# First feed-forward product of quarters 2 to 4 by Strassen's algorithm, with weight sums made in DRAM

## Chip, cores and metric

The kernel runs on one core of a Trainium2 chip (trn2). The metric is the device time of one execution in microseconds (us), median of three runs; TensorE is called PE, VectorE DVE, ScalarE ACT, GpSimd POOL and SyncE SP, as in the profile.

## What is computed

One layer of a streaming encoder on a residual stream x of 512 frames by 1024 channels: a root-mean-square norm, one wide projection, three gated branches (gated linear attention, forgetting attention, attention into 256 memory tokens), a merge with an output projection, and then the feed-forward part, which the change rewrites:

```python
u2 = rmsnorm(h, g_ffn[l])
h = h + jnp.square(jax.nn.relu(u2 @ w_ff1[l])) @ w_ff2[l]
...
return rmsnorm(h, g_final)
```

Here `u2` is 512 x 1024, `w_ff1` 1024 x 4096 and `w_ff2` 4096 x 1024, all float32.

## The kernel before

**Numbers in two halves.** Every large float32 product is made of three PE passes. An operand is split into a rounded half `hi` and a rest `lo`: `split` (L174 to L176) and `split_w` (L112 to L117) make `hi` by a cast on ACT and `lo` by a subtraction on DVE. `mm3` (L122 to L125) then issues hi times hi, hi times lo and lo times hi into one PSUM bank. In the profile these are the lines L123, L124 and L125.

**Weights.** The host lays all weights out as chunks of 128 x 1024 float32 (512 KB), in the order of `chunk_list` (L33). `load_w` (L106) fetches a chunk on SP's queue into one of three `raw` buffers; the halves go into three `hi` and three `lo` buffers of the pool `weights`. A cast therefore waits until PE has finished with the chunk three places back. The matmuls are in the order of the program text; the order on the other engines, their DMA issues included, is set by the framework's planner, and each engine works through its own list strictly in that order.

**Stages.** Memory projection, forgetting attention (`fox_*`, with its projections woven in by `weave`), memory attention woven with the first gated branch, linear attention (`pool("gla")`, L641) woven with the second, then the third branch and the output projection `w_out` (L790 to L851), and then the feed-forward part (from L861). POOL has little to do: in the linear attention it takes the powers in `rsqrt` (L203), clears score tiles (L716) and adds up branches (L571); later it takes the powers of `rms_tile` (L785) and issues accumulating DMAs (L931, L960).

**Into the feed-forward part.** `u2_turn(t)` (L825) transposes the normed rows of one 128-frame tile on PE in two groups and splits each group into `u2h` and `u2l` straight from PSUM. `half` (L836) makes the first two 128-channel tiles of the first product in two halves of 256 frames, so that PE has work while the last frames are normed.

**The feed-forward part** is cut into four quarters of 1024 hidden channels (L983). In each quarter the first product is eight channel tiles, each one weight chunk and 24 matmuls with the weights standing in the array and 512 frames moving (`gT`, L127). `act_evac` (L880) applies relu and square on ACT, forms the seven left factors that the second product needs (L895) and splits them into `ch` and `cl`. Then `second(q)` (L949) makes the second product by Strassen's algorithm: seven products in the order 1, 2, 5, 6, 7, 4, 3, each made of two chunks (called i = 0 and 1) and two row tiles (t), that is 24 matmuls with 512 moving columns; products 1 and 5 stay in PSUM over the quarters. The right factors are sums of blocks of `w_ff2`, and `factor` (L955) forms them in place: POOL issues a DMA that adds a second block from DRAM onto the raw block (L960), and `split_b` (L870) splits the result. Product 6 uses the same raw block as product 5, so its DMA can be issued only when product 5's split has read it. `split_b` puts every fourth chunk into a pair of its own (`bhi`, `blo`), so that a chunk's halves are free again after four chunks.

**The end.** `evac` (L914) adds the products onto the residual rows `hN`; in the last quarter some of these additions are accumulating DMAs (L931). `finish` (L899) makes the sum of squares on ACT, the power on POOL and the scaled output on DVE (L905), and sends two halves out on two queues. Product 3 is last, so the rows t = 0 and 1 are the last to be finished.

Of the kernel before, what the change touches and what calls it, by code (L numbers as in the profile page):

```python
# [32 lines left out]
def chunk_list():  # L33
# [28 lines left out]
def hybrid_block(ctx, tc, chunks, wst, xT, memT, xN, cols, gffn, gfin, wup, cst, out):  # L62
# [42 lines left out]

    def load_w(key, eng=None):  # L106
        i = index[key]
        raw = wp.tile([P, 1024], F32, tag="raw", name=nm("raw"))
        (eng or nc.sync).dma_start(raw, wst[i])
        return raw  # L110

    def split_w(raw):  # L112
        hi = wp.tile([P, 1024], F32R, tag="hi", name=nm("whi"))
        lo = wp.tile([P, 1024], F32R, tag="lo", name=nm("wlo"))
        nc.scalar.copy(hi, raw)  # L115
        nc.vector.tensor_tensor(lo, raw, f(hi), op=ALU.subtract)  # L116
        return hi, lo  # L117
# [670 lines left out]
    u2h = up.tile([P, KT, S], F32R, tag="uhi", name="u2h")  # L788
    u2l = up.tile([P, KT, S], F32R, tag="ulo", name="u2l")
    with pool("outp") as op_:  # L790
# [4 lines left out]
        run(branch("gate_gla", "w_gla_o", ogh, ogl, 2, last=(mh, ml)))  # L795

# [28 lines left out]
        def u2_turn(t):  # L825
            for g in range(2):
# [3 lines left out]
                sl = slice(t * P, (t + 1) * P)  # L830
                last = split(u2h[:, 4 * g:4 * g + 4, sl], u2l[:, 4 * g:4 * g + 4, sl], pt)
# [4 lines left out]
        def half(j, i, ks=range(KT)):  # L836
            sl = slice(256 * i, 256 * i + 256)
            for k in ks:
                mm3(first[j][:, sl], ws[j][0][:, k, :], ws[j][1][:, k, :], u2h[:, k, sl], u2l[:, k, sl], k == 0, k == KT - 1)
# [12 lines left out]
    mst.close()  # L852
# [7 lines left out]

    with pool("ff") as yp:  # L861
        R6, R7 = ([yp.tile([P, 512], F32, name=f"R{n}{t}") for t in range(2)] for n in (6, 7))
        NQ = 4
        held = {}
        split_n = [0]

        def scratch():
            return yp.tile([P, S], F32, tag="sq", name=nm("sq"), bufs=3)

        def split_b(raw):  # L870
            split_n[0] += 1
            own = split_n[0] % 4 == 0
# [3 lines left out]
            return [t.rearrange("p (k c) -> p k c", k=2) for t in (hi, lo)]  # L876

        A = []

        def act_evac(ps):  # L880

            sq = scratch()
            nc.scalar.activation(sq, ps, AF.Relu)
            nc.scalar.activation(sq, sq, AF.Square)
            if not A or A[-1][2] is not None:
                h, l = (yp.tile([P, 7, 256], F32R, tag=g, name=nm(g), bufs=4) for g in ("ch", "cl"))
                split(h[:, 0, :], l[:, 0, :], sq[:, :256])
                A.append([h, l, None, sq])
                return
            h, l, _, sa = A[-1]  # L890
            A[-1][2] = sq
            split(h[:, 1:3, :], l[:, 1:3, :], sq.rearrange("p (a t) -> p a t", a=2))
            ss = yp.tile([P, 4, 256], F32, tag="ss", name=nm("ss"))
            a11, a21, a12, a22 = sa[:, :256], sa[:, 256:], sq[:, :256], sq[:, 256:]
            for o, x, y in ((0, a21, a22), (2, a11, a21), (1, a11, ss[:, 0, :]), (3, a12, ss[:, 1, :])):  # L895
                nc.vector.tensor_tensor(ss[:, o, :], x, y, op=ALU.subtract)
            split(h[:, 3:7, :], l[:, 3:7, :], ss)

        def finish(t, c, n):  # L899
            sumsq(scratch(), hN[t], t, c, n)  # L900
            if n == 1:
                r = rms_tile(yp, t)
                for g, eng in ((0, nc.scalar), (1, nc.sync)):
                    gs_ = slice(512 * g, 512 * g + 512)
                    nc.vector.scalar_tensor_tensor(hN[t][:, gs_], hN[t][:, gs_], r, gl[:, gs_], op0=ALU.mult, op1=ALU.mult)  # L905
                    eng.dma_start(out[t * P:(t + 1) * P, gs_], hN[t][:, gs_])
# [4 lines left out]
        def add(to, x, op=ALU.add):  # L911
            nc.vector.tensor_tensor(to, to, x, op=op)

        def evac(q, n, t, ps):  # L914
            last = q == NQ - 1
            if n == 1 and last:
                add(C(0, 0, t), ps)
            if n in (6, 7):
# [5 lines left out]
            if n == 6 and last:  # L924
                if t == 0:
                    held["G"] = yp.tile([P, 2, 512], F32, tag="ss", name=nm("G"))
                E, G = R6[t], held["G"][:, t, :]
                nc.vector.tensor_tensor(E, held[1][t], R6[t], op=ALU.subtract)
                nc.vector.tensor_tensor(G, held[5][t], E, op=ALU.subtract)
                for to, x in ((C(1, 0, t), E), (C(1, 1, t), G), (C(0, 1, t), G)):  # L930
                    nc.gpsimd.dma_start(to, x, accum_op=ALU.add)  # L931
            if n == 7 and last:
                add(C(1, 1, t), R7[t], ALU.subtract)
                finish(2 + t, 1, 0)
                add(C(1, 0, t), R7[t])
# [4 lines left out]
            if n == 3:  # L940
                add(C(0, 1, t), ps)
                if last:
                    finish(t, 1, 1)
            if n == 2:
                add(C(0, 0, t), ps)
                if last:
# [133 lines left out]
```

## Time and profile before

| what | value |
|---|---|
| median of 3 runs | 864.08 us (863.69 to 866.55) |
| time of the profiled execution | 865.53 us |
| its span, first to last instruction | 863.7 us |
| PE busy | 847.6 us (98%) |
| DVE, ACT, POOL busy | 493.8 (57%), 403.4 (47%), 88.3 us (10%) |
| granted PE clock, mean | 0.992 |
| first product of the third quarter (from 691.23 us of the span on) | 43.52 us |
| second product of the second quarter (from 653.15 us on) | 38.08 us |

The profiled execution lies 1.8 us above its own span and 1.4 us above the median. A matmul row shows a duration that overlaps with its neighbours, since matmuls are pipelined; what counts is the distance from one start to the next. "Busy" of PE in a window is the covered time, not the work done. A bracket at the end of a row of the time line gives the engine's idle time before that instruction and what ended it.

### The profile page before, as it was taken

The page shows a single profiled execution, that of the slowest core. Times are in us where ns is not written, and L with a number is a line of the kernel's source. Part 1 is how long each engine was busy: PE and PEld are TensorE (multiplying, and loading weights), DVE is VectorE, ACT ScalarE, POOL GpSimd, SP SyncE. Part 2 cuts the span into 40 slices and gives each one's busy share as a digit, 9 for nine tenths or more (in the row PEclk, how much of TensorE's full clock was granted, in tenths as well). Part 3 has the DMA queues.
Part 4 walks back from the last instruction along what each step waited for, and adds up shares of the span by engine and source line. Part 5 has one row for each costly group of instructions (what it writes and reads, how often), then busy time and mean ns, then how long its engine had stood idle before and what let it go on. Part 6 is the DMA issues. An engine that isn't in the chain of part 4 may idle for free.

```text
span 863.7 us, 10684 instructions
## 1 busy us (share of the span) xinstructions
PE 847.6 (98%) x4081; PEld 700.0 (81%) x4081; DVE 493.8 (57%) x812; ACT 403.4 (47%) x640; POOL 88.3 (10%) x96
## 2 busy tenths in 40 slices
PE   8999999999999999999999999999999999999995
PEld 5878788888888888787888889888888888888884
DVE  5684556746444546475443446665556645665577
ACT  7665746745243332232333334655455345535642
POOL 5100000000000011212122100011001100110022
PEclk8999999999999999999999999999999999999999
DMA  8333222221221222124332422958625933791156
GB/s 327 123 112 118 91 98 86 90 76 62 92 92 62 90 74 82 41 74 160 109 122 97 146 74 83 352 113 199 204 83 123 278 126 79 145 276 62 25 104 164
DMA packets 31938, 106.10 MB, mean 123 GB/s; under 512 B 3824, under 2 KB 4624, under 8 KB 31888
## 3 DMA queue, kind: packets, MB, share of 16 engines
q1 hardware_dynamic: 24624, 83.92, 27.2%
q0 software_dynamic: 5472, 18.35, 12.0%
q10 hardware_dynamic: 1792, 3.16, 1.0%
q8 instruction: 32, 0.52, 0.3%
q14 instruction: 18, 0.15, 0.1%
HBM read 101.73 MB, written 2.11 MB: 120 GB/s over the span
## 4 chain that ended last, share of the span: by engine, by line
PE 92%; DVE 3%; ACT 1%; DMA 1%; issue 1%; SPq 0%; POOL 0%; DVEq 0%; POOLq 0%; ACTq 0%
PE mm L123 25%; PE mm L124 25%; PE mm L125 25%; PE a L124 3%; PE a L125 3%; PE a L123 3%; PE a L720 1%; PE a L449 1%; DMA h<-G 1%; DMA cst_s<-in_cst_dram 1%; PE a L737 1%; PE a L480 1%; PE a L479 1%; PE a L731 1%; PE a L447 1%
## 5 line engine op out<-in xcount | busy, mean ns | idle before, releaser
L116 DVE TENSOR_TENSOR wlo<-raw,whi 128x1024 fp32r<-128x1024 f32 x104 | 131.1, 1263 | 141.4 <-ACT whi L115 138.4
L115 ACT CAST whi<-raw 128x1024 fp32r<-128x1024 f32 x104 | 109.4, 1053 | 171.5 <-PE mm L124 127.6
L123 PE MATMUL mm<-uhi,whi 128*128 128x512 f32 x360 | 142.4, 396 | 0.0
L124 PE MATMUL mm<-ulo,whi 128*128 128x512 f32 x360 | 140.7, 391 | 1.4 <-DVE ulo L176 1.4
L125 PE MATMUL mm<-uhi,wlo 128*128 128x512 f32 x360 | 140.5, 390 | 0.0
L123 PE MATMUL mm<-u2h,whi 128*128 128x512 f32 x240 | 93.4, 389 | 0.0
L124 PE MATMUL mm<-u2l,whi 128*128 128x512 f32 x240 | 93.4, 389 | 0.0
L125 PE MATMUL mm<-u2h,wlo 128*128 128x512 f32 x240 | 93.4, 389 | 0.0
L124 PEld LDWEIGHTS mm<-ulo,whi 128*128 128x128 f32 x360 | 67.7, 188 | 15.8 <-DVE ulo L176 2.9
L125 PEld LDWEIGHTS mm<-uhi,wlo 128*128 128x128 f32 x360 | 67.6, 188 | 14.5 <-DVE wlo L116 0.4
L176 DVE TENSOR_TENSOR lo<-raw,hi 128x1024 fp32r<-128x1024 f32 x42 | 51.2, 1224 | 48.0 <-ACT hi L175 47.4
L123 PEld LDWEIGHTS mm<-uhi,whi 128*128 128x128 f32 x360 | 67.7, 188 | 13.5 <-issue 0.7
L175 ACT CAST hi<-raw 128x1024 fp32r<-128x1024 f32 x42 | 44.0, 1052 | 61.2 <-PE mm L124 23.5
L960 POOL DMA_DIRECT2D raw<-in_wst_dram x32 | 28.1, 879 | 277.1 <-DVE lo L176 193.6
L124 PEld LDWEIGHTS mm<-u2l,whi 128*128 128x128 f32 x240 | 45.0, 188 | 9.4
L123 PEld LDWEIGHTS mm<-u2h,whi 128*128 128x128 f32 x240 | 45.0, 188 | 9.3
L125 PEld LDWEIGHTS mm<-u2h,wlo 128*128 128x128 f32 x240 | 45.0, 188 | 9.3
L123 PE MATMUL mm<-hi,ch 128*128 128x512 f32 x120 | 46.7, 389 | 0.0
L124 PE MATMUL mm<-lo,ch 128*128 128x512 f32 x120 | 46.7, 389 | 0.0
L125 PE MATMUL mm<-hi,cl 128*128 128x512 f32 x120 | 46.7, 389 | 0.0
L571 POOL TENSOR_TENSOR acc<-acc,th 128x512 f32<-128x512 f32 x16 | 24.1, 1505 | 102.7 <-DVE th L570 102.7
L649 POOL MEMSET qpos<- 64x512 f32 x2 | 1.1, 525 | 269.8 <-PE mm L125 269.7
(316 smaller groups left out, 1646.0 us busy)
## 6 DMA issues: line engine op xcount, KB each, us to landing
raw<-in_wst_dram SPq DMA_DIRECT2D x144, 512.0 KB, 3.3
raw<-in_wst_dram POOLq DMA_DIRECT2D x32, 512.0 KB, 5.3
xr<-in_xT_dram SPq DMA_DIRECT2D x4, 512.0 KB, 8.1
nFb<-dF ACTq DMA_DIRECT2D x8, 256.0 KB, 3.4
h<-in_xN_dram SPq DMA_DIRECT2D x4, 512.0 KB, 7.9
memr<-in_memT_dram SPq DMA_DIRECT2D x4, 256.0 KB, 4.8
h<-G POOLq DMA_DIRECT2D x4, 256.0 KB, 5.7
out_dram<-h ACTq DMA_DIRECT2D x4, 256.0 KB, 2.1
```

What stands on the lines that cost most here:

```text
L115: nc.scalar.copy(hi, raw)
L116: nc.vector.tensor_tensor(lo, raw, f(hi), op=ALU.subtract)
L123: nc.tensor.matmul(ps, lh, rh, start=start, stop=False)
L124: nc.tensor.matmul(ps, lh, rl, start=False, stop=False)
L125: nc.tensor.matmul(ps, ll, rh, start=False, stop=stop)
L175: nc.scalar.copy(hi, src)
L176: return nc.vector.tensor_tensor(lo, src, f(hi), op=ALU.subtract).ins
L447: nc.tensor.matmul(ps[:, :w], q, K[e][:, 0, :w], start=True, stop=False)
L449: nc.tensor.matmul(ps[:, :w], q, K[e][:, 1, :w], start=False, stop=True)
L479: nc.tensor.matmul(po[:, q0:], vv, PTh[:, c0:c0 + w], start=n == 0, stop=False)
L571: nc.gpsimd.tensor_tensor(acc[j], acc[j], th, op=ALU.add)
L960: nc.gpsimd.dma_start(raw[to, i], wst[index["B", q, i, x]], accum_op=ALU.add)
```

## The change

**First product.** Quarter 1 keeps the plain form (`plain_tile`). In quarters 2 to 4 `first_product(q, i)` makes each half of the quarter (512 hidden channels) as a 2 x 2 block product by Strassen's algorithm: seven products in the order 1, 2, 5, 6, 3, 7, 4, each one weight chunk with 24 matmuls of 256 moving columns (two channel tiles a, four k steps, three passes). A half thus takes 7 chunks and 168 matmuls of 256 columns, where four tiles took 4 chunks and 96 matmuls of 512. `first_evac` combines the products from PSUM, applies relu and square, and makes the left factors of the second product as soon as their parts are there.

**Weight sums.** The sums of `w_ff1` blocks for products 4 to 7 are made in DRAM (`tsum`), by 24 DMAs on POOL's queue (12 copies and 12 accumulating ones, 1 MB each), one at every second weight split from the ninth on; each waits for that split's cast (`next_sum`).

**The right sides for it.** `u2_turn` also copies its transposed group unsplit into `b11`, `b12` (one more ACT copy a group); `u2_sums` and `u2_last` make and split the sums of `u2` during quarter 1. The `u2` tiles are laid out in 256-frame blocks.

**Second product.** Its order becomes 1, 2, 5, 6, 3, 7, 4. Of the left factors, three are formed later, during products 1, 2 and 5 of the same quarter. Only two of the four raw blocks are held (`b11`, `b12`); those of products 2 and 3 come through the weight buffers. `split_b` has no pair of its own any more: three buffers for all chunks, while the raw buffers become four.

**The end.** Product 4 is last. In the last quarter products 1, 2 and 3 are added onto `hN` by accumulating DMAs as well, and the rows t = 0, 1 are finished a product earlier, with a multiplication on POOL.

```diff
+    L += [("T", "w_ff1", P * j) for j in range(8)]
     for q in range(4):
-        L += [("T", "w_ff1", P * (8 * q + j)) for j in range(8)]
-        L += [("B", q, i, b) for b in ("11", "21", "12", "22") for i in range(2)]
+        L += [(kind, q, i, b) for kind in ("FB" if q else "B") for b in ("11", "21", "12", "22") for i in range(2)]
...
+    tsum = {(n, q): dram.tile([2, P, 1024], F32, name=f"T{n}_{q}") for q in range(1, 4) for n in (1, 2, 3, 4)}
+    def sum_ops():
+        for q in range(1, 4):
+            for n, src, add in ((1, "11", 0), (3, "12", 0), (1, "12", 1), (3, "22", 1), (2, 1, 0), (2, "22", 1), (4, 2, 0),
+                                (4, "21", 1)):
+                i = index["F", q, 0, src] if isinstance(src, str) else None
+                yield tsum[n, q], tsum[src, q] if i is None else wst[i:i + 2], add
...
+    def next_sum(after):
+        chunk_n[0] += 1
+        op = next(sums, None) if chunk_n[0] > 8 and chunk_n[0] % 2 else None
+        if op is not None:
+            to, src, add_ = op
+            if add_:
+                d = nc.gpsimd.dma_start(to, src, accum_op=ALU.add, max_dma_last_dim=8192)
+            else:
+                d = nc.gpsimd.dma_start(to, src)
+            tc.add_manual_dep(d.ins, after.name, ...)
...
-        nc.scalar.copy(hi, raw)
+        cast = nc.scalar.copy(hi, raw)
         nc.vector.tensor_tensor(lo, raw, f(hi), op=ALU.subtract)
+        next_sum(cast.ins)
...
-                last = split(u2h[:, 4 * g:4 * g + 4, sl], u2l[:, 4 * g:4 * g + 4, sl], pt)
+                last = split(*(x[:, 2 * g + t // 2, :, sl] for x in u2), pt)
+                nc.scalar.copy(plain[t // 2, g].rearrange("p (k t) -> p k t", k=4)[:, :, sl], pt)
...
-            hi, lo = ((yp if own else wp).tile([P, 1024], F32R, tag=g, name=nm(g), bufs=1 if own else 3)
-                      for g in (("bhi", "blo") if own else ("hi", "lo")))
+            hi, lo = (wp.tile([P, 1024], F32R, tag=g, name=nm(g)) for g in ("hi", "lo"))
...
+        def ring(src):
+            load_n[0] += 1
+            raw = (yp if load_n[0] % 4 == 0 else wp).tile([P, 1024], F32, tag="raw", name=nm("raw"))
+            nc.sync.dma_start(raw, src)
+            return split_b(raw)
...
+        def late_left(i):
+            sub(s1[i], ev[i][:, 1, :], od[i][:, 1, :])
+            left(i, 2, s1[i])
+            sub(s1[i], ev[i][:, 0, :], s1[i])
+            left(i, 3, s1[i])
...
+        def first_evac(n, i, ps):
...
+            if n == 1:
+                nc.scalar.copy(a21, ps)
+            if n == 2:
+                nc.vector.tensor_tensor(a11, a21, ps, op=ALU.add)
+                relu2(a11)
+                left(i, 0, a11)
+            if n == 5:
+                nc.scalar.copy(a22, ps)
+            if n == 6:
+                sub(a21, a21, ps)
+                sub(a22, a22, a21)
+            if n == 3:
+                nc.vector.tensor_tensor(a12, a22, ps, op=ALU.add)
+                relu2(a12)
+                left(i, 1, a12)
+            if n == 7:
+                sub(a22, a22, ps)
+                add(a21, ps)
+                relu2(a22)
+            if n == 4:
+                add(a21, ps)
+                relu2(a21)
+                late_left(i)
...
+        def first_product(q, i):
+            for n in ORDER:
...
+                ps = mmt([P, 2, 256])
+                for a in range(2):
+                    for k in range(4):
+                        mm3(ps[:, a, :], wh[:, a, k, :], wl[:, a, k, :], uh[:, s, k, :], ul[:, s, k, :], k == 0, k == 3)
+                first_evac(n, i, ps)
...
         def finish(t, c, n):
             sumsq(scratch(), hN[t], t, c, n)
+            early = n == 0 or t < 2
+            if early:
+                (nc.gpsimd if t < 2 else nc.vector).tensor_tensor(h[c], h[c], g_[c], op=ALU.mult)
             if n == 1:
                 r = rms_tile(yp, t)
-                for g, eng in ((0, nc.scalar), (1, nc.sync)):
-                    gs_ = slice(512 * g, 512 * g + 512)
-                    nc.vector.scalar_tensor_tensor(hN[t][:, gs_], hN[t][:, gs_], r, gl[:, gs_], op0=ALU.mult, op1=ALU.mult)
-                    eng.dma_start(out[t * P:(t + 1) * P, gs_], hN[t][:, gs_])
+                for x in range(2):
+                    if x != c or early:
+                        nc.scalar.mul(h[x], h[x], r)
+                    else:
+                        nc.vector.scalar_tensor_tensor(h[x], h[x], r, g_[x], op0=ALU.mult, op1=ALU.mult)
+                    (nc.scalar if x != c else nc.sync).dma_start(out[t * P:(t + 1) * P, 512 * x:512 * x + 512], h[x])
...
+        def factor(q, n, i):
+            if n in (2, 3):
+                return ring(wst[index["B", q, i, {2: "21", 3: "22"}[n]]])
+            to, x = {1: (b11, None), 5: (b11, "12"), 6: (b11, "22"), 7: (b12, "22"), 4: (b11, "21")}[n]
+            if x is not None:
+                send(to[i], wst[index["B", q, i, x]])
+            return split_b(to[i])
...
+                for i in range(2):
+                    if n == 1:
+                        sub(od[i][:, 0, :], od[i][:, 0, :], s1[i])
+                        left(i, 0, od[i][:, 0, :])
+                    if n == 2:
+                        sub(ev[i][:, 1, :], ev[i][:, 0, :], ev[i][:, 1, :])
+                        left(i, 1, ev[i][:, 1, :])
+                    if n == 5:
+                        left(i, 2, od[i][:, 1, :])
...
+        second_product(0)
+        for q in range(1, NQ):
+            first_product(q, 0)
+            load_blocks(q)
...
+            first_product(q, 1)
+            second_product(q)
```

More of the change, by code (lines that the diff above doesn't have):

```diff
@@ L795, in hybrid_block @@
         run(branch("gate_gla", "w_gla_o", ogh, ogl, 2, last=(mh, ml)))
+        mst.close()
+        bp = ctx.enter_context(pool("blocks", side="right"))
+        b11, b12 = ([bp.tile([P, 1024], F32, name=f"b{n}{i}") for i in range(2)] for n in ("11", "12"))
+        plain = {(0, 0): b11[0], (0, 1): b11[1], (1, 0): b12[0], (1, 1): b12[1]}
         def res_evac(c):
@@ L916, in evac @@
             if n == 1 and last:
-                add(C(0, 0, t), ps)
-            if n in (6, 7):
+                x = scratch()
+                nc.scalar.copy(x, ps)
+                send(C(0, 0, t), x)
+                sub(R6[t], x, R6[t])
+            if n == 2:
+                if last:
+                    x = scratch()
+                    nc.scalar.copy(x, ps)
+                    send(C(0, 0, t), x)
+                else:
+                    add(C(0, 0, t), ps)
+            if n in (6, 7) and not last:
                 R = (R6 if n == 6 else R7)[t]
@@ L968, in second @@
                     ps = held.setdefault(n, [at_() for _ in range(2)] if q == 0 else None)
[L969 to L972 removed]
+                end = q == NQ - 1 and n == ORDER[-1]
+                for js in ([[0, 1]] if end else [[0], [1]]):
+                    w = {i: [x.rearrange("p (k c) -> p k c", k=2) for x in factor(q, n, i)] for i in js}
                     for t in range(2):
@@ L998, in hybrid_block @@
                 nc.sync.dma_start(gl, gfin)
-            second(q)
+                for t in range(2):
+                    add(C(1, 0, t), R7[t])
+                    add(C(1, 1, t), R7[t], ALU.subtract)
+            first_product(q, 1)
+            second_product(q)
 def layout(inputs):
```

188 lines of the change are left out of this document (111 added, 77 removed).

## Prediction, made before the changed kernel was run

> **What bounds the kernel now.** I read the page's busy times, the chain, the busy times by window and the time line, in this order.
>
> ```profile
> PE 847.6 (98%) x4081; PEld 700.0 (81%) x4081; DVE 493.8 (57%) x812; ACT 403.4 (47%) x640; POOL 88.3 (10%) x96
> PEclk8999999999999999999999999999999999999999
> PE 92%; DVE 3%; ACT 1%; DMA 1%; issue 1%; SPq 0%; POOL 0%; DVEq 0%; POOLq 0%; ACTq 0%
> ```
>
> PE covers nearly the whole span and 92% of the chain, at full clock. Busy PE is not yet PE at its pace, so I look at distances. Two windows (us, then PE, PEld, DVE, ACT, POOL), the first product of the third quarter and the second product of the second:
>
> ```profile
> 691.23:734.75 43.52, 43.52 (x193) 36.04 (x192) 22.75 (x33) 22.98 (x33) 1.75 (x2) 1.00 0.35 104
> 653.15:691.23 38.08, 38.08 (x169) 31.53 (x168) 24.98 (x28) 17.43 (x18) 5.25 (x6) 1.00 0.78 205
> ```
>
> 192 weight loads (one a matmul) in 43.52 us are 226.7 ns a matmul; 168 in 38.08 us are 226.7 ns too. Both stages run at one pace from start to end: PE never waits, and only fewer or shorter matmuls can shorten them.
>
> **PE's work.** A quarter's first product falls from 192 matmuls of 512 columns to 14 x 24 = 336 of 256. In columns that is 7/8. The pace of 256 columns is in the trace, in the two tiles made in halves:
>
> ```profile
> 526.86 0.28 PE L123 MATMUL mm<-u2h,fhi 128*128 128x256 f32 x1
> ...
> 529.98 0.28 PE L125 MATMUL mm<-u2h,flo 128*128 128x256 f32 x1
> L123 PEld LDWEIGHTS mm<-u2h,fhi 128*128 128x128 f32 x32 | 6.1, 191 | 0.0
> 531.62:538.88 7.26, 7.26 (x63) 7.26 (x62) 4.69 (x5) 1.51 (x3) 0.00 (x0) 1.00 0.64 201
> ```
>
> Line by line 26 steps lie between the first two rows: 3.12 us / 26 = 120.0 ns. Twice that is 240, not 227: a matmul has a fixed part of some 13 ns, and halving the columns pays it twice. 336 x 120.0 = 40.32 us, against 43.52: **-3.20 us a quarter, -9.6 us** for three, well under the eighth (-16.3). The last row (60 halves' matmuls, 121 ns) gives -8.6 as the other end. The second product keeps its 168 matmuls. The weight load's own row says 191 ns, and yet matmuls follow at 120: loads overlap each other or the matmuls.
>
> [...]
>
> **What the other engines must do behind it.** Rows of one operation each:
>
> ```profile
> L176 DVE TENSOR_TENSOR lo<-raw,hi 128x1024 fp32r<-128x1024 f32 x42 | 51.2, 1224 | 48.0 <-ACT hi L175 47.4
> L175 ACT CAST hi<-raw 128x1024 fp32r<-128x1024 f32 x42 | 44.0, 1052 | 61.2 <-PE mm L124 23.5 <-DMA raw<-in_wst_dram 23.3 <-PE mm L125 9.5
> L912 DVE TENSOR_TENSOR h<-h,mm 128x512 f32<-128x512 f32 x24 | 15.8, 680 | 6.3 <-PE mm L125 6.3
> L175 ACT CAST ch<-sq 128x512 fp32r<-128x512 f32 x16 | 9.9, 622 | 0.5
> L884 ACT ACTIVATE sq<-sq 128x512 f32<-128x512 f32 x32 | 20.2, 633 | 1.0
> ```
>
> A half (7 chunks, 20.16 us of PE) costs DVE 7 x 1.22 for the rests, plus 13 operations of 512 columns (one each after products 2, 3; two after 6, 7; one after 4, two subtractions in late_left, four rests) x 0.68: 8.6 + 8.8 = 17.4 us. ACT: 7 x 1.05, two copies and eight relu or square x 0.63, four casts x 0.62: 16.2 us. So 86% and 80% busy, where the old first product had 53% each. Both still fit. A chunk's cast can start when PE leaves the chunk three places back; it is needed two chunks (5.76 us) later, and cast plus rest take 2.3 us. The fullest step (after product 4) puts 1.22 + 5 x 0.68 = 4.6 us on DVE against 2.88, 1.7 us over, within the 3.4 us spare, and the next step (product 1, only a copy on ACT) gives it back. The products turn through four PSUM tiles, so an evacuation may be three products late. I take +0.7 us for all six halves; the ends are 0 and 13.8 (each half waits once for a whole split, 2.3 us). In the second product DVE has 14 x 1.22 + 20 x 0.68 = 30.7 of 38.1 us.
>
> **The wait that grows.** Product 6 splits the raw block on which product 5 was split; its DMA is issued when product 5's rest is done. Second quarter, i = 0, then the first quarter's:
>
> ```profile
> 657.16 1.23 DVE L176 TENSOR_TENSOR lo<-raw,hi 128x1024 fp32r<-128x1024 f32 x1
> 658.68 0.88 POOL L960 DMA_DIRECT2D raw<-in_wst_dram  x1 [12.96 <-DVE lo L176]
> 663.89 1.05 ACT L175 CAST hi<-raw 128x1024 fp32r<-128x1024 f32 x1 [4.04 <-DMA raw<-in_wst_dram]
> 664.97 1.23 DVE L176 TENSOR_TENSOR lo<-raw,hi 128x1024 fp32r<-128x1024 f32 x1 [1.41 <-ACT hi L175]
> 669.70 0.39 PE L124 MATMUL mm<-lo,ch 128*128 128x512 f32 x1
> ...
> 584.24 1.23 DVE L176 TENSOR_TENSOR lo<-raw,hi 128x1024 fp32r<-128x1024 f32 x1 [2.28 <-ACT hi L175]
> 588.10 0.39 PE L124 MATMUL mm<-lo,ch 128*128 128x512 f32 x1
> DMA to landing us min/median/max: 5.0/5.3/11.7
> ```
>
> The rest is ready at 666.20 and used at 669.70: 3.5 us spare; in the first quarter 2.6. Now four buffers become three: product 5's split starts one chunk (12 matmuls, 2.72 us) later, so the spare shrinks to +0.8 and -0.1. New left-factor work (two subtractions, two rests, two casts) falls in the same stretch. What stands behind a late landing: the waiting cast on ACT, behind it every later cast and relu; DVE's rest; PE. I take +0.5 us a quarter. In the last quarter products 1 and 2 send four more 256 KB additions through the same queue:
>
> ```profile
> q0 software_dynamic: 5472, 18.35, 12.0%
> q1 hardware_dynamic: 24624, 83.92, 27.2%
> ```
>
> 12.0% of 863.7 us for 18.35 MB is 5.65 us a MB, 1.5 us for one such addition: +1.5 there. Sum **+3 us**, ends 0 and 4 x 6.4 = 25.6 (every landing at 11.7).
>
> **Weight sums.** 24 DMAs of 1.05 MB. At those shares an accumulating one takes 5.9 us of all 16 engines, a copy 2.9: 12 x 8.8 = 106 us, spread over 46 chunks of at least 24 matmuls (5.44 us), thus 250 us or more. Who waits there now:
>
> ```profile
> DMA  8333222221221222124332422958625933791156
> ACT whi L115 <- PE mm L124: 127.6, 57, 9.3
> ACT whi L115 <- DMA raw<-in_wst_dram: 5.0, 2, 3.3
> ```
>
> The DMA engines stand at 0.2 to 0.4 in that stretch, and casts wait for PE to free buffers, hardly ever for a load: cover enough. If it were gone, a load late by one long landing would cost up to 11.7 us. On POOL, powers and branch additions queue behind a sum's issue (0.88 us) and its wait; behind the power stand DVE's scaling and then PE's transposes, some steps later. I take +0.3.
>
> **Entry.** Two more ACT copies (0.58 us each) per frame tile stand near the last norm:
>
> ```profile
> 526.79 0.58 ACT L175 CAST u2h<-a 128x512 fp32r<-128x512 f32 x1
> 527.27 0.63 ACT L777 ACTIVATE hsq<-h 128x512 f32<-128x512 f32 x1
> 529.11 1.41 DVE L807 SCALAR_TENSOR_TENSOR un<-h,rr,gf 128x512 f32<-128x512 f32 x2
> 530.83 0.38 PE L829 MATMUL a<-cst_s,un 128*128 128x128 f32 x2
> ```
>
> The last `un` is ready at 530.52, 0.3 us ahead of PE. One copy ahead of the sum of squares costs 0.58 - 0.3: **+0.3** (0 to 0.9). The sums of u2 (3 x 2.4 + 2 x 0.68 = 8.6 us of DVE) lie beside the plain tiles (24 x 0.2267 = 5.4 us each, four of them).
>
> **The end.**
>
> ```profile
> 854.20 0.39 PE L125 MATMUL mm<-bhi,cl 128*128 128x512 f32 x1
> 854.50 1.41 DVE L905 SCALAR_TENSOR_TENSOR h<-h,rr,gl 128x512 f32<-128x512 f32 x2
> 855.95 0.67 DVE L912 TENSOR_TENSOR h<-h,mm 128x512 f32<-128x512 f32 x1
> 858.44 0.55 POOL L785 TENSOR_TENSOR rr<-ms,cst_s 128x1 f32<-128x1 f32 x1 [1.72 <-DVE ms L784]
> 859.02 1.41 DVE L905 SCALAR_TENSOR_TENSOR h<-h,rr,gl 128x512 f32<-128x512 f32 x2 [0.73 <-POOL rr L785]
> ```
>
> The last addition starts 1.4 us after PE's last matmul has ended (854.59), behind two scalings; then come squares, power, two scalings, output. Afterwards one scaling stands in the way instead of two (-0.7), the two last run on two engines (-0.7), and fewer outputs are left: -1.5. Against it, POOL's four multiplications for rows 0 and 1 must be out of the last power's way, and they start only when product 3's additions have landed.
>
> ```profile
> 37.70 1.29 POOL L337 TENSOR_TENSOR ut<-xr,rxb 128x512 f32<-128x512 f32 x1 [6.02 <-ACT rxb L213]
> 37.66 2.55 DVE L339 SCALAR_TENSOR_TENSOR ut<-xr,cols_s,rxb 128x512 f32<-128x512 f32 x2 [2.24 <-ACT rxb L213]
> ```
>
> A POOL multiplication takes 1.29 us, and two DVE operations beside it took 2.55 us where two alone take 1.41 (529.11): 1.1 us lost. [...] One collision and one multiplication ahead of the power (1.1 + 1.3) would turn -1.5 into +0.9; I take **-1.5**, ends -3 and +1.
>
> **Sum.** -9.6 + 0.7 + 3.0 + 0.3 + 0.3 - 1.5 = **-6.8 us**. Against the profiled execution's 865.5 (span 863.7 and 1.8 around it) that is 858.7; it lies 1.4 above the median of 864.1, so the forecast is **857.3**.
>
> **Rivals.**
> 1. *Eaten by the lists.* DVE and ACT at over 80% in strict order make PE wait one cast (1.05 us) in each of the six halves: -6.8 + 6.3 gives 863.6. For it: cast and rest alternate between the engines; against it: 3.4 us spare.
> 2. *Slower: the DMA of product 6 lands late.* With the spare gone, each us of landing over 5.3 counts four times. At 8.5 us it costs 4 x 3.2 = 12.8: 870.1. It decides from 7.0 us (6.8 / 4 = 1.7 over the median). For it: the engines at 0.78 in that window, the 11.7; against it: the landings quoted were about 5 us.
> 3. *It doesn't do what it says:* 256 columns don't hold 120 ns with semaphores at each product. From 43.52 / 336 = 129.5 ns nothing is gained; at the load's 191 ns a quarter takes 64.2 us, +62 in all, 926. Against it: the rows above. [...]
> 4. *The sums hold up POOL or the loads* by one long landing: 857.3 + 11.7 = 869.
>
> **Chances.** Forecast 0.64, rival 1 0.15, rival 2 0.13, rival 3 0.03, rival 4 0.05. A difference of 0.3% (2.6 us) is what a measurement of this kernel can tell from no change. Faster 0.64, within 0.15, slower 0.21. The range goes down to 852 (end at -3, no stalls at all: 864.1 - 12.6 = 851.5) and up to 867, half way into rival 2.
>
> **What would show it.** Right: 336 matmuls of 256 columns in 40.3 to 41.5 us a quarter; DVE near 85% there; the chain still over 90% PE; product 6 starting within 1 us of product 5's end; 6 to 8 us from the last matmul to the end. Wrong: waits of PE for `lo` at products 5 to 6, or for `wl` in the first product; POOL waiting for its own sums; casts waiting for loads between the ninth and 55th split.

## Result and the profile after

Twelve runs of the changed kernel beside twelve of the old one on one chip gave 864.61 us against 863.88 (medians; 863.11 to 867.84 and 861.62 to 867.5). The ratio is 1.0013, with a 95% interval of 0.9999 to 1.0027: no change that can be measured, where 857.3 us were forecast. The profiled execution took 864.26 us, its span 862.5.

The page of the changed kernel (busy times; the chain; two lines of DMA issues, whose last number is the median time in us from issue to landing):

```profile
PE 839.0 (97%) x4513; PEld 711.2 (82%) x4513; DVE 542.4 (63%) x850; ACT 440.3 (51%) x703; POOL 113.0 (13%) x130
...
PE 74%; issue 12%; DMA 6%; DVE 3%; ACT 2%; POOL 1%; SPq 0%; POOLq 0%; ACTq 0%; DVEq 0%
...
b<-in_wst_dram POOLq DMA_DIRECT2D x32, 512.0 KB, 5.3
T<-in_wst_dram POOLq DMA_DIRECT2D x12, 1024.0 KB, 8.4
```

PE is still busy 97% of the span, yet it holds only 74% of the chain, where it held 92%. 6% of the chain now is one thing: additions by DMA to the blocks `b`. They land after 5.3 us in the median, as before, so in the median it is not their length that is new but when they are issued.

Windows of the changed kernel by stage (us, length, then PE, PEld, DVE, ACT, POOL, granted clock, DMA share): second product of quarter 1, first and second product of quarter 2, second products of quarters 3 and 4, and the end from the start of PE's last matmul.

```profile
568.34:606.72 38.38, 38.37 (x169) 31.45 (x168) 27.38 (x32) 22.53 (x29) 5.17 (x6) 1.00 0.78 186
606.72:647.04 40.32, 40.32 (x338) 40.31 (x337) 32.29 (x39) 28.02 (x38) 0.86 (x1) 1.00 0.62 204
647.04:685.89 38.85, 38.40 (x170) 31.46 (x169) 30.00 (x37) 20.04 (x24) 6.03 (x7) 1.00 0.84 200
...
726.20:765.78 39.58, 38.72 (x170) 31.46 (x169) 31.22 (x39) 20.15 (x24) 6.03 (x7) 1.00 0.81 192
...
806.10:848.48 42.38, 40.34 (x170) 32.32 (x168) 29.98 (x40) 23.25 (x36) 15.79 (x18) 0.96 0.81 143
848.48:862.46 13.98, 0.39 (x2) 0.00 (x0) 4.69 (x10) 6.49 (x16) 6.53 (x8) 0.64 0.40 151
```

The first product gained what was forecast: 336 matmuls in 40.32 us instead of 192 in 43.52. The second products, all 38.08 or 37.85 before, grow from quarter to quarter, though PE has the same 168 matmuls in each; and the end, 9.53 us before (854.20 to 863.73), is 13.98. The balance:

| stage | before | after | difference |
|---|---|---|---|
| three first products | 3 x 43.52 | 3 x 40.31 | -9.6 |
| four second products | 38.08, 38.08, 38.08, 37.85 | 38.39, 38.85, 39.58, 42.38 | +7.1 |
| end | 9.53 | 13.98 | +4.5 |
| 200th matmul to the feed-forward part (all weight sums) | 479.68 | 479.74 | +0.1 |
| entry and quarter 1's first product | 45.12 | 45.12 | 0 |
| start to the 200th matmul | 46.75 | 43.48 | -3.3 |

The lengths are distances between starts of matmuls in the two traces. The last row has nothing to do with the change: over the profiled executions of all twelve kernels here that stretch lies between 42.4 and 46.8 us, whatever the edit. It goes with the granted clock, which over that stretch is 0.89 before and 0.96 after: 0.89 x 46.75 and 0.96 x 43.48 come to 41.6 and 41.7 us at full clock. Without it the changed kernel is 2.0 us longer. So the whole gain was given back and a little more, some 60% of it in the second products and the rest at the end.

**Where PE waits.** The waits of PE in the four second products of the changed kernel (total us, times, longest):

```profile
PE mm L152 <- DVE lo L204: 2.5, 4, 0.8
PE mm L151 <- ACT hi L203: 0.8, 1, 0.8
```

All five stand at product 6. They show 3.3 us of the 7.1, since matmul rows overlap (0.39 us long, 0.227 apart) and hide a part of each gap. By the distances from start to start, beyond the usual 0.227 us, the gaps at product 6 come to about 5.2 us; the other 1.9 us are slow matmuls, which the last section shows. The time line of quarter 3 shows one with its history (the rest of product 5's first chunk, the DMA that it releases, product 6's cast and rest, and the matmul):

```profile
733.25 1.22 DVE L204 TENSOR_TENSOR lo<-b,hi 128x1024 fp32r<-128x1024 f32 x1
...
734.77 0.86 POOL L1050 DMA_DIRECT2D b<-in_wst_dram  x1 [7.06 <-DVE lo L204]
...
741.71 1.05 ACT L203 CAST hi<-b 128x1024 fp32r<-128x1024 f32 x1 [4.01 <-DMA b<-in_wst_dram]
...
742.80 1.23 DVE L204 TENSOR_TENSOR lo<-b,hi 128x1024 fp32r<-128x1024 f32 x1 [2.98 <-ACT hi L203]
...
744.08 0.50 PE L152 MATMUL mm<-lo,ch 128*128 128x512 f32 x1 [0.76 <-DVE lo L204]
```

The rest is there at 744.03; PE had ended product 5 at 742.5. In the old kernel the same rest was 3.5 us early (quarter 2). One such miss costs the lateness of the cast and then up to 1.03 us more, because PE takes `hi` first and then stands again until the rest has followed the cast.

In quarters 1 and 2 product 6's additions landed within 5.1 to 5.3 us, and the late one was that of its second chunk. Quarter 2 (cast and rest of product 5's second chunk, the DMA that the rest releases, and the matmul):

```profile
655.73 1.04 ACT L203 CAST hi<-b 128x1024 fp32r<-128x1024 f32 x1
...
657.63 1.22 DVE L204 TENSOR_TENSOR lo<-b,hi 128x1024 fp32r<-128x1024 f32 x1
...
659.14 0.86 POOL L1050 DMA_DIRECT2D b<-in_wst_dram  x1 [2.68 <-DVE lo L204]
...
666.94 0.50 PE L152 MATMUL mm<-lo,ch 128*128 128x512 f32 x1 [0.45 <-DVE lo L204]
```

The rest began 0.86 us after the cast had ended: DVE was still busy with left factors and an addition. The DMA went out 12.1 us after the quarter's start, where the old kernel has 8.25 (661.40): 3.85 us later, of which the lost pair, one chunk, explains 2.72. So the lost pair and the new left-factor work act together here.

**The last quarter** adds ACT's copies for the sends to the list ahead of product 5's split, and ends in a longer miss:

```profile
811.76 0.59 ACT L1056 COPY sq<-a 128x512 f32<-128x512 f32 x1 [0.37 <-PE a L153]
812.25 1.05 ACT L203 CAST hi<-b 128x1024 fp32r<-128x1024 f32 x1
...
818.08 0.86 POOL L1050 DMA_DIRECT2D b<-in_wst_dram  x1
...
825.79 1.05 ACT L203 CAST hi<-b 128x1024 fp32r<-128x1024 f32 x1 [3.24 <-DMA b<-in_wst_dram]
...
826.89 0.49 PE L151 MATMUL mm<-hi,ch 128*128 128x512 f32 x1 [0.76 <-ACT hi L203]
828.15 0.57 PE L152 MATMUL mm<-lo,ch 128*128 128x512 f32 x1 [0.76 <-DVE lo L204]
```

That addition landed 7.6 us after its issue. The matmuls stand 1.15 and 1.26 us apart instead of 0.23, and after them comes something new, which the last section shows: nine matmuls at up to 0.43 us.

**The end.** The changed kernel around the end of product 4 (POOL's row of 4.20 us is three multiplications):

```profile
843.30 0.86 POOL L1050 DMA_DIRECT2D h<-sq  x1 [1.92 <-issue]
...
845.42 0.68 DVE L1036 TENSOR_TENSOR h<-h,gl 128x512 f32<-128x512 f32 x1
...
846.67 0.63 ACT L805 ACTIVATE sq<-h 128x512 f32<-128x512 f32 x1 [1.53 <-DMA h<-sq]
...
847.48 4.20 POOL L1036 TENSOR_TENSOR h<-h,gl 128x512 f32<-128x512 f32 x3 [3.32 <-ACT sq L805]
848.85 1.71 DVE L1036 TENSOR_TENSOR h<-h,gl 128x512 f32<-128x512 f32 x1
850.86 0.68 DVE L913 TENSOR_TENSOR h<-h,mm 128x512 f32<-128x512 f32 x1
851.64 0.56 POOL L813 TENSOR_TENSOR rr<-ms,cst_s 128x1 f32<-128x1 f32 x1
...
852.24 1.33 ACT L1041 ACTIVATE h<-h,rr 128x512 f32<-128x512 f32 x2 [1.77 <-POOL rr L813]
853.48 0.61 ACT L805 ACTIVATE sq<-h 128x512 f32<-128x512 f32 x1
```

Read it upwards: the last square waits on ACT behind scalings that wait for a power; the power waits on POOL behind three multiplications; these wait for a square that waits for a send issued at 843.30. The last addition, at 850.86, had its matmuls by 848.9; a DVE multiplication of 1.71 us instead of 0.68 stood ahead of it, beside POOL's. The 0.68 us is that of 845.42, with no operation of POOL beside it; in run 1 two such multiplications beside POOL's took 1.53 and 0.92 us.

The end's +4.45 us has three parts. From the start of PE's last matmul to the end of the last scaling it is 8.3 us instead of 6.2 (+2.1). From there to SyncE's last step, which comes 0.4 us after the last output has landed (860.32; before, 862.52), it is 3.8 us instead of 2.5 (+1.35): six of the eight outputs now go out between 854.83 and 856.85, where the old kernel sent a pair about every 2.2 us (853.35, 855.27, 857.54, 859.80), and the last one lands 3.5 us after its issue instead of 2.1. What follows that step grew by 1.0 us, from 0.8 to 1.8 (last section).

### The profile page after: what moved, and what is told of

It is laid out like the page before. It is cut to its first block, busy times and chain, and to the rows that moved or that the text cites. A ratio compares the mean times of both kernels' runs of the same rounds, so it can differ in the third digit from the quotient of the medians.

```text
span 862.5 us, 11811 instructions
## 1 busy us (share of the span) xinstructions
PE 839.0 (97%) x4513; PEld 711.2 (82%) x4513; DVE 542.4 (63%) x850; ACT 440.3 (51%) x703; POOL 113.0 (13%) x130
## 4 chain that ended last, share of the span: by engine, by line
PE 74%; issue 12%; DMA 6%; DVE 3%; ACT 2%; POOL 1%; SPq 0%; POOLq 0%; ACTq 0%; DVEq 0%
PE mm L152 20%; PE mm L153 20%; PE mm L151 20%; DMA b<-in_wst_dram 6%; PE a L151 2%; PE a L152 2%; PE a L153 2%; ACT hi L203 1%; PE a L748 1%; DVE lo L204 1%; PE a L477 1%; DMA cst_s<-in_cst_dram 1%; PE a L765 1%; PE a L508 1%; PE a L507 1%
## 5 line engine op out<-in xcount | busy, mean ns | idle before, releaser
L143 DVE TENSOR_TENSOR wlo<-raw,whi 128x1024 fp32r<-128x1024 f32 x80 | 101.7, 1275 | 104.1 <-ACT whi L142 103.5
L204 DVE TENSOR_TENSOR lo<-b,hi 128x1024 fp32r<-128x1024 f32 x40 | 48.9, 1223 | 38.3 <-ACT hi L203 38.2
L203 ACT CAST hi<-b 128x1024 fp32r<-128x1024 f32 x40 | 41.9, 1048 | 57.5 <-PE mm L153 24.1
L1050 POOL DMA_DIRECT2D b<-in_wst_dram x32 | 27.7, 865 | 267.1 <-DVE lo L204 210.2
L152 PE MATMUL mm<-u2l,hi 128*128 128x256 f32 x192 | 54.3, 283 | 0.0
L153 PE MATMUL mm<-u2h,lo 128*128 128x256 f32 x192 | 54.3, 283 | 0.0
L151 PE MATMUL mm<-u2h,hi 128*128 128x256 f32 x192 | 54.3, 283 | 0.0
L151 PE MATMUL mm<-u2sh,hi 128*128 128x256 f32 x144 | 40.8, 283 | 0.0
L152 PE MATMUL mm<-u2sl,hi 128*128 128x256 f32 x144 | 40.8, 283 | 0.0
L153 PE MATMUL mm<-u2sh,lo 128*128 128x256 f32 x144 | 40.8, 283 | 0.0
```

Source lines behind the costliest of these rows:

```text
L151: nc.tensor.matmul(ps, lh, rh, start=start, stop=False)
L152: nc.tensor.matmul(ps, lh, rl, start=False, stop=False)
L153: nc.tensor.matmul(ps, ll, rh, start=False, stop=stop)
L203: nc.scalar.copy(hi, src)
L204: return nc.vector.tensor_tensor(lo, src, f(hi), op=ALU.subtract).ins
```

## Experiments

**The theory** is that products 5 and 6 in a row use one block, that with three pairs of halves product 5's split comes too late for product 6's DMA, and that at the end the sends and POOL's multiplications set the time. **The rivals** are that the left factors made meanwhile, or the sends, are the load that delays the splits; and at the end that the new order itself is the cause. Each median below stands beside that of the old kernel, run in the same group, and each ratio is to it. Experiments 1 to 6 have twelve runs each, 7 to 10 four to six.

**1. Without the extra sends.**

```diff
-                x = scratch()
-                nc.scalar.copy(x, ps)
-                send(C(0, 0, t), x)
-                sub(R6[t], x, R6[t])
+                add(C(0, 0, t), ps)
+                sub(R6[t], ps, R6[t])
```

Products 2 and 3 are treated likewise.

> The changed kernel, but in the last quarter products 1, 2 and 3 are added onto the residual rows by DVE straight from PSUM, as before the change, so six of the twelve accumulating DMAs of 256 KB and their ACT copies are gone. Theory A (those additions, their copies and subtractions delay product 6's DMA in the last quarter): the last second product falls from 42.6 us to about 39.5, as in the third quarter, and the end, from the last matmul's start to the last instruction, from 14.0 to 12 or 13 us, since the rows 0 and 1 wait for nothing on POOL's queue; total 4 to 5 us under the changed kernel. Rival B (three pairs of halves alone make product 6 late): the last second product stays over 41.5 us and the total within 1.5 us of the changed kernel.

862.75 us against 863.26 of the old kernel, ratio 0.9989 (0.9973 to 1.0006). The last second product fell from 42.38 to 40.77 us, between the two theories, the others stayed near theirs (38.46, 38.66, 39.25), the end went to 13.14. POOL's multiplications alone hold it:

```profile
844.44 4.66 POOL L1036 TENSOR_TENSOR h<-h,gl 128x512 f32<-128x512 f32 x3 [9.33 <-ACT sq L805]
...
844.76 1.53 DVE L1036 TENSOR_TENSOR h<-h,gl 128x512 f32<-128x512 f32 x1
```

**2. With the old finish**, the sends kept.

```diff
-            if early:
-                (nc.gpsimd if t < 2 else nc.vector).tensor_tensor(h[c], h[c], g_[c], op=ALU.mult)
...
+                for g, eng in ((0, nc.scalar), (1, nc.sync)):
+                    nc.vector.scalar_tensor_tensor(hN[t][:, gs_], hN[t][:, gs_], r, gl[:, gs_], op0=ALU.mult, op1=ALU.mult)
```

> The changed kernel with the end of before: no multiplication on POOL, both halves of a row tile scaled on DVE once the power is there. Theory A (POOL's four multiplications and ACT's six scalings make the end long): the end falls from 14.0 us to about 10.5, total 3 to 3.5 us under the changed kernel, second products unchanged. Rival B (the late landing of product 3's additions sets the end): the end stays over 13 us and the total within 1 us of the changed kernel.

864.32 us, 1.0015 (0.9998 to 1.0031), end 12.98 us: now the sends of product 3, landed at 848.8, hold it. Each list holds the last scaling by itself: it ends 8.0 us after the start of PE's last matmul in both runs, 8.3 with both lists and 7.2 with neither (run 5), so neither run alone could show that gain. With the old finish the outputs go out in pairs again, and SyncE's last step comes 2.35 us after the last scaling instead of 3.8 (4.1 in run 1); but here GpSimd's closing drain (last section) ends 1.8 us after that step.

**3. Product 6's right factor summed in DRAM ahead of time** like the weight sums, so that it waits for no block.

```diff
+            if n == 6:
+                return ring(b6[q][i])
```

> The changed kernel, but product 6's right factor is summed in DRAM beforehand too (12 more DMAs of 1 MB on POOL's queue, at the even splits) and loaded like the factors of products 2 and 3; product 4 gets both additions instead, so the number of DMAs inside the second products is the same. Theory A (what grew is the wait of product 6 for a DMA that can start only after product 5's split): second products of 38.1 to 38.4 us in the first three quarters and 39 to 40 in the last, total 5 to 6 us under the changed kernel. Rival B (DVE's and ACT's fuller lists in the second products hold PE, whatever the DMA does): second products stay at 38.4, 38.9, 39.6 and over 41.

865.54 us, 1.0021 (1.0003 to 1.0039). Quarters 1 and 2 went back to 38.08 and 38.11 us with three pairs, and the last one fell from 42.38 to 38.44, which shows that the wait at product 6 is the loss there. But product 4 now needs two additions in a row and stood late in quarter 3 (40.76), and the end grew to 15.85.

**4. The old kernel with three pairs of halves.**

```diff
-            own = split_n[0] % 4 == 0
+            own = False
```

> The kernel before with three pairs of halves for the right factors in the place of four, nothing else. By the spare times of the prediction (2.6 to 3.5 us less 2.7) theory A expects second products longer by 0 to 0.4 us each and a total within 1.5 us of the kernel before: the buffers alone are not enough, it takes the added left-factor work beside them. Rival B (the buffers alone are the cause): second products of 39 to 40 us, 4 to 7 us in all.

865.08 us, 1.0021 (1.0001 to 1.004). Second products 38.08, 38.57, 38.08, 39.01: the lost pair costs the old kernel 1.65 us, and the changed one loses 7.1. In the last quarter (+1.16) this is more than theory A had, in all far less than the rival's 4 to 7. The pair alone is not all; it took away the slack in which the new lists would have fitted.

**5. Both end edits (1 and 2) together.**

> The changed kernel without the extra sends of products 1, 2 and 3 in the last quarter and with the old finish (VectorE scales each row block in one operation, GpSimd multiplies nothing). Theory A, each of the two new lists is enough to set the end by itself: with both gone the end is 9.5 to 10.5 us (13.1 and 13.0 with one of them gone), the last second product about 40.8 us as without the sends, total 858 to 860 us. Rival B, the order of the last quarter sets the end (six sums of squares on ScalarE come only after product 7): the end stays at 12.5 us or more, total 861 to 863 us.

862.41 us against 862.75 in that group, 1.0004 (0.999 to 1.0018). The end is 11.71 us, between the two theories; 1.3 us of it are GpSimd's closing drain, after SyncE's last step. The second products stay at 38.57, 38.81, 39.65 and 41.02.

**6. Product 7 ahead of product 6**, on top of 5; the last quarter's additions follow that order.

```diff
-            for at, n in enumerate(ORDER):
+            for at, n in enumerate((1, 2, 5, 7, 6, 3, 4)):
```

> As the run with both ends, and the second products in the order 1, 2, 5, 7, 6, 3, 4, so that no two products in a row wait for an addition by DMA to the same block. Theory A, the second products lose their time because product 6's block can be sent only after product 5's is read: they take 38.1 to 38.5 us each, also the last, and the end stays at 9.5 to 10.5 us: total 854.5 to 857 us. Rival B, the three pairs of halves (four before) and the left factors' lists on VectorE and ScalarE set the pace: the second products stay at 38.4, 38.7, 39.2 and 40.5 us or more, total as the run with both ends, within 1 us.

862.4 us, 0.9994 (0.9976 to 1.0012), runs from 859.4 to 867.45. My theory that the order is the cause fell here: the waits left product 6, but the profiled execution, the slowest of the twelve, has them at product 4. Quarter 1's window, then POOL's last issues in it and the casts of product 4's two chunks:

```profile
569.30:612.30 43.00, 40.21 (x169) 32.59 (x168) 27.69 (x32) 22.54 (x29) 5.23 (x6) 0.96 0.77 185
```
```profile
588.24 1.75 POOL L1043 DMA_DIRECT2D b<-in_wst_dram  x2 [6.16 <-DMA b<-in_wst_dram]
591.11 1.75 POOL L1043 DMA_DIRECT2D b<-in_wst_dram  x2 [1.12 <-DMA b<-in_wst_dram]
...
598.10 1.05 ACT L203 CAST hi<-b 128x1024 fp32r<-128x1024 f32 x1 [0.81 <-DMA b<-in_wst_dram]
605.77 1.04 ACT L203 CAST hi<-b 128x1024 fp32r<-128x1024 f32 x1 [6.62 <-DMA b<-in_wst_dram]
```

In each POOL row the first of the two issues waits for a load of its block, so it belongs to product 7 of the next quarter, whose block is free early in this order; the second is product 4's. Four additions stand in the queue within 4 us, and product 4's last one, issued by 592.9, is landed only at 605.77. In the last quarter, with no next one behind it, the same order takes 37.9 us. So with three pairs the new order moved the late addition to another product in this execution instead of removing it; the faster executions were not traced.

**7. The fourth pair back**, on top of 5, in the changed order.

```diff
-            hi, lo = (wp.tile([P, 1024], F32R, tag=g, name=nm(g)) for g in ("hi", "lo"))
+            split_n[0] += 1
+            own = split_n[0] % 4 == 0
+            hi, lo = ((yp if own else wp).tile([P, 1024], F32R, tag=g, name=nm(g), bufs=1 if own else 3)
+                      for g in (("bhi", "blo") if own else ("hi", "lo")))
```

> As the run with both ends, in the changed kernel's order, with the fourth pair of halves back (the room for it comes from one buffer of the throw-away outputs of the squares). Theory A (product 6's block): the fourth pair gives at most 0.3 us a quarter, the third second product stays at 39 us or more and the last at 40 or more; total 858 to 860 us. Rival B (pairs of halves): the second products fall to 38.1 to 38.4 us, the last to 39, total 855.5 to 857.5 us.

857.6 us, 0.994 (0.9928 to 0.9952). Second products 38.08, 38.11, 38.11, 39.39: the rival on the pairs was right, the theory of product 6's block as the only cause was not.

**8. Both: order and pair.**

> Product 7 before product 6, the fourth pair of halves, and both ends as before the change. If either theory alone is the whole cause, this is as fast as the better of the two runs, within 0.7 us; if each has a part, it is faster than both: second products 38.1 to 38.2 us, end 9.5 to 10.5 us, total 854 to 856 us.

855.97 us, 0.9925 (0.9912 to 0.9938); the last second product falls to 37.88, so with the pair the order has its part too. The end is 12.11, where 9.5 to 10.5 were expected.

**9. G added by DVE**, on top of 8.

```diff
-                for to, x in ((C(1, 0, t), E), (C(1, 1, t), G), (C(0, 1, t), G)):
-                    send(to, x)
+                send(C(1, 0, t), E)
+                add(C(1, 1, t), G)
+                add(C(0, 1, t), G)
```

> As the run with the order 1, 2, 5, 7, 6, 3, 4 and the fourth pair, but in the last quarter VectorE adds G to the two blocks, and only E goes by DMA (two sends where there were six). Theory A, the end is 12.1 us instead of 9.5 because the four scalings of two row blocks, which waited for sends that landed at 839.8 and 842.4, stand on VectorE ahead of the last additions: the end falls to 9 to 10 us, the last second product stays under 38.3 us, total 852.8 to 854 us. Rival B, VectorE's eight more operations in product 6 hold up the rests behind them: the last second product grows by 1 to 3 us, and the total is 855 us or more.

855.13 us against 861.9 in that group, 0.9911 (0.9889 to 0.9933): the fastest version here, faster than both kernels, if by less than theory A had it (its profiled execution took 854.5). Its last second product and its end:

```profile
804.67:842.55 37.88, 37.88 (x170) 31.35 (x168) 35.65 (x55) 21.76 (x35) 5.79 (x8) 1.00 0.46 79
842.55:852.73 10.18, 0.38 (x2) 0.00 (x0) 4.90 (x9) 0.72 (x2) 1.60 (x3) 0.76 0.54 207
```

DVE is busy 35.65 of 37.88 us and holds nothing up (the edit adds four operations to it, not the eight of the expectation: 864 against 860); the end lost 1.9 us by the sends that went.

**10. The changed kernel with the fourth pair back**, and the sends' source moved to make room for it.

> The changed kernel with the fourth pair of halves as its only difference (the sends of the last quarter read from R7, so that the throw-away buffer can be one). Theory A, the lost fourth pair is what the second products of quarters 1 to 3 lose: they go back to 38.1 us each, the last to 40.5 to 41, the end stays at 13 to 14 us, total 859.5 to 861.5 us. Rival B, the late sends fill the queue also here and the last quarter keeps its 42.4 us: total 861.5 to 863 us.

859.04 us, 0.9954 (0.9936 to 0.9971), so 0.5% faster than the old kernel, with its end still at 14.29 us. Windows of the second products of quarters 1, 3 and 4, and the time line of quarter 3 to set beside the changed kernel's:

```profile
569.71:607.79 38.08, 38.08 (x169) 31.54 (x168) 27.48 (x32) 22.66 (x29) 5.17 (x6) 1.00 0.83 196
...
726.53:764.63 38.10, 38.10 (x170) 31.54 (x169) 31.20 (x39) 20.16 (x24) 5.17 (x6) 1.00 0.84 211
804.95:843.74 38.79, 38.17 (x169) 31.27 (x168) 28.25 (x39) 22.20 (x34) 15.18 (x18) 1.00 0.82 140
```
```profile
731.11 1.22 DVE L204 TENSOR_TENSOR lo<-b,hi 128x1024 fp32r<-128x1024 f32 x1
...
732.63 0.86 POOL L1054 DMA_DIRECT2D b<-in_wst_dram  x1 [8.32 <-DVE lo L204]
...
737.98 1.05 ACT L203 CAST hi<-b 128x1024 fp32r<-128x1024 f32 x1 [1.92 <-DMA b<-in_wst_dram]
...
739.06 1.23 DVE L204 TENSOR_TENSOR lo<-b,hi 128x1024 fp32r<-128x1024 f32 x1 [1.26 <-ACT hi L203]
```

Counted from the quarter's start (726.53 here, 726.20 there) the DMA is issued at 6.1 us instead of 8.6, close to one chunk (2.72 us) earlier, and lands after 5.35 us instead of 6.9. The rest is done at 13.8 us, where it was 17.8; product 6 begins at 16.3. A spare of 2.6 us stands against a miss of 1.5, with the same work on DVE (31.20 and 31.22 us) and ACT. In the last quarter the same sends go through the same queue for 38.79 us where they took 42.38.

Here the sends cost nothing that shows, less than either side expected: run 7, which has the pair and not these sends, needs 39.39 us. That the spare takes them up is likely, but not shown.

The lengths side by side, in us (the last column leaves out the start up to the 200th matmul):

| kernel | second products | end | 200th matmul to end |
|---|---|---|---|
| before | 38.08, 38.08, 38.08, 37.85 | 9.53 | 817.0 |
| after | 38.39, 38.85, 39.58, 42.38 | 13.98 | 819.0 |
| 5, both ends | 38.57, 38.81, 39.65, 41.02 | 11.71 | 815.5 |
| 10, pair alone | 38.08, 38.11, 38.11, 38.79 | 14.29 | 813.1 |
| 7, ends and pair | 38.08, 38.11, 38.11, 39.39 | 11.95 | 811.4 |
| 8, and order | 38.08, 38.11, 38.11, 37.88 | 12.11 | 810.1 |
| 9, and DVE | 38.08, 38.11, 38.11, 37.88 | 10.19 | 808.1 |

## Why the prediction was wrong

- **PE's work: right.** -9.6 us forecast, -9.6 measured; 256 columns keep 120 ns. Rival 3 is out.
- **The lists in the first product: too careful.** +0.7 forecast, 0 measured: DVE 32.29 and ACT 28.02 of 40.32 us, and PE without a gap. Rival 1 is out as a mechanism; that the total ended near its 863.6 is chance.
- **The wait that grows: the step that failed, by its size.** The mechanism and its place were right: four buffers to three, the DMA of product 6 issued a chunk later, PE waiting for `lo` between products 5 and 6. But I priced what was left as +0.5 a quarter and took +3 us in all; it measured +0.31, +0.77, +1.50 and +4.53, together 7.1. The spare was worked out for product 6's first chunk alone and priced as if nothing else moved. For that chunk it was near enough (0.4 us in quarter 2, where +0.8 was forecast). The second chunk, whose spare the sum left out, missed by 0.55 us there, with its DMA 3.85 us later instead of 2.72, because the split of product 5's second chunk stood behind the new left-factor work. In quarter 3 the landing grew too (6.9 us where the run with the pair has 5.35), and behind a late cast came the second wait of up to 1.03 us for the rest. The last quarter's +1.5 for the sends was too small as well: copies ahead of product 5's split, a landing of 7.6 us, and then 1.9 us of half clock, which no term had. Runs 4 and 10 show the cause: with the pair back, 6.1 of the 7.1 us go, and without it the old work loses only 1.65, so it takes the lost pair and the new work together.
- **Rival 2** had the same place with a wrong trigger: the median landing stayed at 5.3 us, and the chance hung on landings of 7 us or more; only one of product 6's eight, in the last quarter, reached that.
- **Weight sums: right in kind.** +0.3 forecast, +0.1 measured from the 200th matmul to the feed-forward part; the 12 accumulating DMAs, with a median landing of 8.4 us, and the 12 copies (5.3 to 5.8 us) stand there under cover. One sign of being wrong came without harm: POOL waited once, 9.0 us, for one of its own sums. Rival 4 is out.
- **Entry: nothing instead of +0.3.** The planner put the square ahead of the new copies, so the norm did not wait:

```profile
524.59 0.65 ACT L805 ACTIVATE hsq<-h 128x512 f32<-128x512 f32 x1
...
525.68 0.61 ACT L864 COPY b<-a 128x512 f32<-128x512 f32 x1
```

- **The end: wrong by its sign.** -1.5 forecast, +4.45 measured. The prediction named the danger, POOL's multiplications ahead of the last power, and priced it at one collision and one multiplication (+0.9 in all); there were four multiplications, three of them ahead of the power at 851.64, one of DVE's took 1.71 us and one of POOL's too, and they started only when a send had landed that was issued at 843.30. That is +2.1 us up to the last scaling. The "fewer outputs" of the -1.5 went the wrong way as well: with the new finish they crowd, +1.35 us. Runs 1, 2 and 5 show that sends and multiplications each hold the end by themselves (13.14 and 12.98 us), that without both 11.71 remain, and that the old finish takes the outputs' part back; run 9 shows that sends of G are 1.9 us of what is left on top of run 8. The last 1.0 us of the +4.45 is GpSimd's closing drain (below).

With the two failed terms at their measured size the sum is -9.63 + 7.11 + 4.45 + 0.06 = +2.0 us, as the traces have it from the 200th matmul on; the runs' medians, which hold the changing start as well, differ by +0.7.

## What to carry to other kernels

When a change takes away a buffer, work out for each chain that runs through it how early its last step is now, and treat a spare of less than one transfer's spread (here 5.3 to 7.6 us) as a loss, not as nothing: the same new work cost 7.1 us with three pairs and 1 us with four. Where several lists end together, as at the end here, one edit at a time shows little: 0.8 and 1.0 us for the two lists, 2.3 for both. The pair alone brought 0.5% over the old kernel; 0.9% took the pair, the order and the end together. And a faster first stage is worth what the stage behind it can still feed.

## What the runs showed of the hardware

**After a stall of about 2 us PE's granted clock was 0.50 for 3.41 us.** In the last quarter of the changed kernel, after the two gaps quoted above (0.92 and 1.03 us beyond the usual distance), the time line and the window of the same stretch read:

```profile
829.37 0.63 PE L152 MATMUL mm<-lo,ch 128*128 128x512 f32 x1
829.79 0.63 PE L153 MATMUL mm<-hi,cl 128*128 128x512 f32 x1
...
831.90 0.39 PE L152 MATMUL mm<-lo,ch 128*128 128x512 f32 x1
832.13 0.39 PE L153 MATMUL mm<-hi,cl 128*128 128x512 f32 x1
```
```profile
828.10:831.70 3.60, 3.55 (x9) 2.80 (x10) 3.46 (x4) 1.16 (x2) 0.87 (x1) 0.55 0.53 86
```

Nine matmuls follow each other at up to 0.427 us instead of 0.227, at a granted clock of 0.55 in this window (0.50 from 828.43 to 831.85, 1.00 ahead of it and after it): 1.9 us on top of the stall. The order run (6) shows the same after stalls of 3.2 us (quarter 1, 43.00 us at a mean clock of 0.96) and 2.1 us (quarter 2, 42.00 us at 0.96), and not after 2.2 us in quarter 3 (40.40 us at 1.00).

So the length of a stall alone does not decide; what else does was not tested. The other stretches at 0.50 in the changed kernel's trace are from 12.65 to 16.06 us, again 3.41 long, and from 852.33 to the end; in the old kernel's they are from 13.24 to 20.07, from 30.31 to 33.72 and from 859.75 to the end.

**GpSimd's closing drain grew.** The trace records it with 3.8 us in the old kernel (858.41 to 862.18, before SyncE's last step at 862.96) and 6.2 in the changed one (855.45 to 861.67, after SyncE's at 860.70). It thus became the last thing, and adds about 1 us to the end. Why it is longer was not tried.
